# Weight sums a step earlier and on VectorE, a first operand in halves, and squares two steps later, in a decoder trunk on one core

## The chip, the cores and the metric

The kernel runs on one core of a Trainium2 chip. The metric is the device time of one execution in microseconds (us); three executions of the kernel before gave 2124.61, 2126.71 and 2128.39 us, so its median is 2126.71 us. The engines are named as the profile names them: PE (TensorE, PEld its weight loads), DVE (VectorE), ACT (ScalarE), POOL (GpSimd) and SP (SyncE, which issues most of the DMAs).

## The reference

Two layers on a stream `h` of 1024 tokens by 1024 features, all in float32: a gated short convolution with a feed-forward, then latent attention with a feed-forward, and a last norm.

```
def short_conv_mixer(h, w_in, conv_w, w_out):
    gate_b, gate_c, val = jnp.split(h @ w_in, 3, axis=-1)
    z = gate_c * val
    conv = sum(conv_w[k] * shifted(z, k) for k in range(3))
    return (gate_b * conv) @ w_out

def swiglu_ffn(h, w13, w2):
    g, u = jnp.split(h @ w13, 2, axis=-1)
    return (jax.nn.silu(g) * u) @ w2

h = h + short_conv_mixer(rms_norm(h), ...);  h = h + swiglu_ffn(rms_norm(h), ...)
h = h + latent attention(rms_norm(h), ...);  h = h + swiglu_ffn(rms_norm(h), ...)
return rms_norm(h, final_norm_g)
```

The attention turns queries and keys by tables `cos` and `sin` of the positions. `shifted` stands for the causal shift by k tokens.

## The kernel before

**Products.** Every matrix product in float32 is made of parts: an operand is split into a high part (a cast on ACT, L111) and a low part (operand less high part, a subtraction on DVE, L112), and three matmuls per tile (L153 to L155: high by high, low by high, high by low) give the product. Large products are further taken as 2 by 2 blocks by a scheme with seven block products in place of eight, whose operands are sums and differences of blocks. So between a loaded weight and the PE stand: a sum of blocks, a cast on ACT, a subtraction on DVE.

**Steps.** The order of all work is written by hand. `Steps` (L266) holds a list of PE steps; a step is one block product of 12 matmuls of 128x512. `before(n, ...)` puts other work ahead of step n and `after(n, ...)` behind it, and `run` emits all of it in that one order. Each engine takes its own instructions strictly in that order, and a wait for another engine holds up everything behind it on the same engine. SP's queue of DMAs is in order as well.

**Up products.** `up` (L487) plans the conv, and the two up projections of the feed-forwards, as `Quad`s of seven products. For a quad it loads two weight tiles `ra` and `rb`, splits one pair as it is (`pair_hi`, `pair_lo`), makes four sums in place (`sum3`, `sum1`, `sum2`, `sum4`, L386 to L396) and splits each by `half` (L398) two steps ahead of the product that reads it. Both `sum2` and `sum4` overwrite a buffer that an earlier half has read. The conv stage has 12 quads (three for each two of eight channel groups); seven of them (`head`) take their first two products ahead of the others, so that each has five steps in a row left. Its first product's operand comes from `block` and `first_block` (L918, L933): the PE transposes a normed tile into PSUM, DVE or ACT scales it (L927, L929), and the operand is split in pieces of 128x1024 (L316, L317). Results of a quad are folded from PSUM by DVE and ACT (`evict`, L445), multiplied and run through the three taps (L826 to L835) or gated (L843), on DVE.

**Down products.** `Down` (L656) makes the two down projections f1 and f2 as seven products of 11 k-tiles in groups of two; a group has its operands loaded (`load_m`, `load_w`) and split (`parts`, tiles mp and wp) two steps ahead of its first step. At the end of a product its four banks are added into the stream (L738), and where a piece of the stream is then complete, `complete` (L536) follows at once: in f1 it stores the piece and, for the second half of the later features, makes parts for the next stage; in f2 it makes the square for the last norm (L768), folds squares (L754) and applies the gain (L1598). In f2 the rows of the first half are normed and stored under the last products (`fnorm.flush`, `out_rows`, `out_turn`, `out_store`, L1657 to L1661).

**Tables.** Under f1's first products the rope tables are made, one small turn per step from step 6 of f1 on (L1153): for each half of the tokens a load of positions (L1093), a conversion (L1096), a reduction of the angle on DVE in some 16 turns, and last `sin` (L1106), which holds four DVE instructions, two sines on ACT (L1112, L1113), a negation on DVE (L1114) and two stores (L1115, L1116).

Of the kernel before, what the change touches and what calls it, by code (L numbers as in the profile page):

```python
# [10 lines left out]
F32R = mybir.dt.float32r  # L11
# [37 lines left out]
def trunk(ctx, tc, aps, out):  # L49
# [437 lines left out]
    def up(steps, quads, op, ahead=0):  # L487
# [20 lines left out]
        for x in quads:  # L508
# [16 lines left out]
            steps.before(n[x, 6] - 2, x.sum2, lambda x=x: x.half(6))  # L525
            steps.before(n[x, 7] - 2, lambda x=x: x.half(7))
            steps.before(n[x, 4] - 2, lambda x=x: x.half(4))
            steps.before(n[x, 3] - 2, x.sum4, lambda x=x: x.half(3))
# [127 lines left out]
    class Down:  # L656
# [12 lines left out]
        def product(self, steps, i):  # L669
# [66 lines left out]
            def evict(q, cb, t, sign):  # L736
                hv = st.h[cb * 4 + q][:, t * 512:(t + 1) * 512]
                nc.vector.tensor_tensor(hv, hv, banks[q], ALU.add if sign > 0 else ALU.subtract)  # L738
                if LAST[cb, t] == i:
                    complete(cb * 4 + q, t, self.final, self.keep)  # L740

            for j, o in enumerate(todo):
                steps.after(s - 3 + o[0] if tail else s + j // 2, lambda o=o: evict(*o))
# [78 lines left out]
    def conv_pair(j):  # L822
# [15 lines left out]
        return Quad(w_in, (KD + j) * P, (2 * KD + j) * P, AF.Copy, [product, first, tap(1), tap(2)], nc.gpsimd)  # L838

    def gate_pair(j):  # L840
        def done(i, c):
            y = kept[i]
            nc.vector.tensor_tensor(y, y, c, ALU.mult)  # L843
            if i < KD - 2:
                nc.sync.dma_start(md["conv"][i], y)
        return Quad(w_in, j * P, (j + 1) * P, AF.Copy, [lambda c1, c2: done(j, c1), lambda c1, c2: done(j + 1, c2)], nc.gpsimd)
# [89 lines left out]

    def first_x():
# [9 lines left out]
        first_block(0, 0)  # L947
# [14 lines left out]

    up(steps, conv_quads, xop)
    steps.before(1, lambda: first_block(1, 0), lambda: first_block(1, 1), xop.advance)
# [114 lines left out]
    def tables(hh):  # L1079
# [26 lines left out]
        def sin():  # L1106
# [4 lines left out]
            nc.vector.tensor_scalar(k, k, -1.0, float(np.pi / 2), ALU.mult, ALU.add)  # L1111
            nc.scalar.activation(x, a, AF.Sin)  # L1112
            nc.scalar.activation(a, k, AF.Sin)  # L1113
            nc.vector.tensor_scalar(x[64:128], x[64:128], -1.0, None, ALU.mult)  # L1114
# [7 lines left out]
        return out + [sin]  # L1122
# [30 lines left out]
    for j, fn in enumerate(tables(0) + tables(1)):  # L1153
        steps.before(dn.start + 6 + j, fn)
# [502 lines left out]
    steps.before(e[4] + 3, lambda: fnorm.flush(0))  # L1657
    steps.before(e[4] + 5, lambda: out_rows(0))
    for tb in range(4):
        for q in range(2):  # L1660
            steps.before(e[4] + 6 + (2 * tb + q + 1) // 2, lambda tb=tb, q=q: (out_turn(tb, q), out_store(tb, q)))  # L1661
# [43 lines left out]
```

## Time and profile before

| what | value |
| --- | --- |
| median of 3 runs (lowest, highest) | 2126.71 us (2124.61, 2128.39) |
| the profiled execution | 2122.53 us |
| its span | 2120.6 us |
| granted clock of PE, mean | 0.995 of full speed |
| PE, DVE, ACT, POOL busy | 97%, 69%, 40%, 15% of the span |
| chain of waits that ended last | PE 83%, DVE 7%, DMA 4%, ACT 3% |

The span is the profiled part of an execution; 1.9 us of its time lie around it. A share of busy time is a mean over stages: conv up from 0 to about 300 us, conv out to 380, f1's up to 787, f1's down to 997, attention to 1455, f2's up to 1880, f2's down to 2113. The bracket in a row of a timeline is the idle time of that engine ahead of the instruction and what ended it. A matmul of 128x512 lasts 0.39 us, and the next starts 0.23 us after it where nothing is late.

### The profile page before, as it was taken

How to read it: one execution, taken by the hardware profiler on the slowest of the kernel's cores; microseconds unless marked ns; L12 is line 12 of the kernel's file. 1: busy time of each engine (PE TensorE's matmuls, PEld its weight loads, DVE VectorE, ACT ScalarE, POOL GpSimd, SP SyncE). 2: the span in 40 equal slices, each digit the busy share in tenths (PEclk: the TensorE clock that was granted, in tenths of full speed). 3: DMA queues.
4: the chain of work that ended last, by engine and by line, in shares of the span. 5: the costliest groups of instructions: out<-in, count | busy, mean ns of one | idle time of the engine just before them, and what ended most of it. 6: DMA issues, size and time to landing. Idle time of an engine off the chain costs nothing.

```text
span 2120.6 us, 25572 instructions
## 1 busy us (share of the span) xinstructions
PE 2066.0 (97%) x9542; PEld 1706.4 (80%) x9542; DVE 1460.6 (69%) x2175; ACT 858.0 (40%) x1439; POOL 315.2 (15%) x412
## 2 busy tenths in 40 slices
PE   7999999999999999999999999989999999999998
PEld 6778888888888887787888888877888888888777
DVE  5787656887666668867577777437886666667555
ACT  7423434433333333354245555225433333333445
POOL 2233200122122210000023232101111111100000
PEclk9999999999999999999999999999999999999999
DMA  7255775586766586564232223325487475685543
GB/s 231 70 120 121 226 269 178 117 204 188 186 165 153 139 286 230 193 226 146 70 69 69 65 63 121 138 79 174 128 200 178 149 169 154 154 322 193 179 148 120
DMA packets 274315, 338.96 MB, mean 160 GB/s; under 512 B 18047, under 2 KB 177984, under 8 KB 273872
## 3 DMA queue, kind: packets, MB, share of 16 engines
q1 hardware_dynamic: 240144, 262.71, 38.1%
q0 software_dynamic: 33888, 74.56, 16.4%
q8 instruction: 74, 1.21, 0.2%
q14 instruction: 49, 0.40, 0.1%
q10 hardware_dynamic: 160, 0.07, 0.0%
HBM read 260.22 MB, written 126.35 MB: 182 GB/s over the span
## 4 chain that ended last, share of the span: by engine, by line
PE 83%; DVE 7%; DMA 4%; ACT 3%; issue 2%; SPq 0%; POOL 0%; DVEq 0%; ACTq 0%; POOLq 0%
PE q L154 16%; PE q L153 16%; PE q L155 16%; PE dn L155 4%; PE dn L154 4%; PE dn L153 4%; PE ps_s L1438 4%; PE pl L155 2%; PE pl L153 2%; PE pl L154 2%; DVE wp_lo L112 1%; PE ps_t L1460 1%; PE ps_l L155 1%; PE ps_l L153 1%; PE ps_l L154 1%
## 5 line engine op out<-in xcount | busy, mean ns | idle before, releaser
L153 PE MATMUL q<-xh,w_hi 128*128 128x512 f32 x1568 | 613.3, 391 | 6.3 <-ACT w_hi L111 2.6
L154 PE MATMUL q<-xl,w_hi 128*128 128x512 f32 x1568 | 611.5, 390 | 2.9 <-DVE xl L317 2.9
L155 PE MATMUL q<-xh,w_lo 128*128 128x512 f32 x1568 | 611.5, 390 | 0.9 <-DVE w_lo L112 0.9
L153 PEld LDWEIGHTS q<-xh,w_hi 128*128 128x128 f32 x1568 | 294.8, 188 | 70.6 <-ACT w_hi L111 3.8
L154 PEld LDWEIGHTS q<-xl,w_hi 128*128 128x128 f32 x1568 | 294.7, 188 | 65.9 <-DVE xl L317 4.8
L155 PEld LDWEIGHTS q<-xh,w_lo 128*128 128x128 f32 x1568 | 294.7, 188 | 63.2 <-DVE w_lo L112 2.4
L112 DVE TENSOR_TENSOR w_lo<-wr,w_hi 128x512 fp32r<-128x512 f32 (+1 forms) x272 | 196.6, 723 | 215.1 <-ACT w_hi L111 214.2
L111 ACT CAST w_hi<-wr 128x512 fp32r<-128x512 f32 (+1 forms) x272 | 170.1, 630 | 372.1 <-DVE wr L390 151.2
L155 PE MATMUL dn<-mp_hi,wp_lo 128*128 128x512 f32 (+1 forms) x628 | 245.3, 391 | 6.3 <-DVE wp_lo L112 4.5
L153 PE MATMUL dn<-mp_hi,wp_hi 128*128 128x512 f32 (+1 forms) x628 | 244.3, 389 | 1.0 <-ACT wp_hi L111 1.0
L154 PE MATMUL dn<-mp_lo,wp_hi 128*128 128x512 f32 (+1 forms) x628 | 243.3, 387 | 0.9 <-DVE mp_lo L112 0.9
L1050 POOL COPY paced<-pace 128x1 f32<-128x1 f32 x128 | 84.8, 663 | 923.0 <-ACT pace L1049 923.0
L112 DVE TENSOR_TENSOR mp_lo<-m,mp_hi 128x1024 fp32r<-128x1024 f32 x84 | 95.3, 1134 | 127.2 <-ACT mp_hi L111 125.6
L111 ACT CAST mp_hi<-m 128x1024 fp32r<-128x1024 f32 x84 | 82.2, 979 | 209.8 <-PE dn L154 204.0
L155 PEld LDWEIGHTS dn<-mp_hi,wp_lo 128*128 128x128 f32 x628 | 118.3, 188 | 38.8 <-DVE wp_lo L112 15.5
L153 PEld LDWEIGHTS dn<-mp_hi,wp_hi 128*128 128x128 f32 x628 | 118.3, 188 | 25.5 <-ACT wp_hi L111 2.8
L154 PEld LDWEIGHTS dn<-mp_lo,wp_hi 128*128 128x128 f32 x628 | 118.4, 188 | 25.5 <-DVE mp_lo L112 1.3
L112 DVE TENSOR_TENSOR wp_lo<-w,wp_hi 128x1024 fp32r<-128x1024 f32 x84 | 94.8, 1128 | 0.0
L111 ACT CAST wp_hi<-w 128x1024 fp32r<-128x1024 f32 x84 | 82.0, 976 | 0.0
L1445 ACT ACTIVATE p<-ps_s,mx,rq 128x128 f32<-128x128 f32 (+3 forms) x64 | 53.3, 834 | 56.6 <-DVE mx L1442 51.4
L382 DVE TENSOR_TENSOR w_lo<-wr,w_hi 128x1024 fp32r<-128x1024 f32 x56 | 68.7, 1226 | 7.6 <-ACT w_hi L378 7.6
L738 DVE TENSOR_TENSOR h<-h,dn 128x512 f32<-128x512 f32 x108 | 68.7, 679 | 0.0
(292 smaller groups left out, 3218.8 us busy)
## 6 DMA issues: line engine op xcount, KB each, us to landing
m<-md_f SPq DMA_DIRECT2D x70, 512.0 KB, 4.9
md_f<-c SPq DMA_DIRECT2D x110, 256.0 KB, 3.4
wr<-in_conv_ffn_w_dram SPq DMA_DIRECT2D x47, 512.0 KB, 5.7
wr<-in_mla_ffn_w_dram SPq DMA_DIRECT2D x47, 512.0 KB, 5.4
w<-mw_f SPq DMA_DIRECT2D x40, 512.0 KB, 3.9
h<-hd SPq DMA_DIRECT2D x32, 512.0 KB, 9.3
wr<-in_conv_w_in_dram SPq DMA_DIRECT2D x31, 512.0 KB, 5.2
mw_f<-in_conv_ffn_w_dram POOLq DMA_DIRECT2D x30, 512.0 KB, 7.2
```

What stands on the lines that cost most here:

```text
L111: nc.scalar.copy(out=hi, in_=src)
L112: (eng or nc.vector).tensor_tensor(lo, src, hi.bitcast(F32), ALU.subtract)
L153: nc.tensor.matmul(ps, lhsT=wh, rhs=xh, start=st, stop=False, **more)
L154: nc.tensor.matmul(ps, lhsT=wh, rhs=xl, start=False, stop=False, **more)
L155: nc.tensor.matmul(ps, lhsT=wl, rhs=xh, start=False, stop=en, **more)
L382: nc.vector.tensor_tensor(lo, self.ra, hi.bitcast(F32), ALU.subtract)
L738: nc.vector.tensor_tensor(hv, hv, banks[q], ALU.add if sign > 0 else ALU.subtract)
L1050: nc.gpsimd.tensor_copy(b, a)
L1438: nc.tensor.matmul(ps[:, a:b], lhsT=q[:, qs], rhs=k[:, a:b], start=i == 0, stop=i == 4)
L1445: nc.scalar.activation(p[:, :kw], ps[:, :kw], AF.Exp, bias=mx, scale=rq[:, qb:qb + 1], accum_out=rsum)
L1460: nc.tensor.transpose(t[:, j * P:(j + 1) * P], ps_[j][:, kb * P:(kb + 1) * P], ident)
```

## The change

It has five parts.

1. `up`: `sum2` and `sum4` stand a step earlier than the halves that they feed, in conv and in both feed-forwards (before: directly ahead of them). They run on DVE as before.
2. `conv_pair` and `gate_pair` (the same edit in both, the diff shows one): `sum3` and `sum1` of the conv stage run on DVE instead of POOL, and one step later (the step depends on the engine in `up`).
3. `first_halves` stands for the first `first_block`: the very first operand is scaled and split in two chunks of 128x512, one by one. The second pair of blocks, `first_block(1, 0)` and `(1, 1)`, is emitted ahead of the next quad's `pair_hi` in the same step.
4. `Down`: `complete` follows two steps behind the addition of a bank (not in the last product of f2), and the flush, rows, turns and stores of f2's first half move two steps later.
5. `tables`: the positions are loaded at steps 2 and 18 of f1 (before: in turn, at steps 6 and 24), and `sin` falls into three turns, a step each: the DVE instructions, the two sines on ACT, the negation with the stores.

```diff
-            steps.before(n[x, 6] - 2, x.sum2, lambda x=x: x.half(6))
+            steps.before(n[x, 6] - 3, x.sum2)
+            steps.before(n[x, 6] - 2, lambda x=x: x.half(6))
...
-            steps.before(n[x, 3] - 2, x.sum4, lambda x=x: x.half(3))
+            steps.before(n[x, 3] - 3, x.sum4)
+            steps.before(n[x, 3] - 2, lambda x=x: x.half(3))
...
-                if LAST[cb, t] == i:
+                if LAST[cb, t] == i and tail:
                     complete(cb * 4 + q, t, self.final, self.keep)
 
             for j, o in enumerate(todo):
-                steps.after(s - 3 + o[0] if tail else s + j // 2, lambda o=o: evict(*o))
+                n = s - 3 + o[0] if tail else s + j // 2
+                steps.after(n, lambda o=o: evict(*o))
+                if LAST[o[1], o[2]] == i and not tail:
+                    steps.after(n + 2, lambda o=o: complete(o[1] * 4 + o[0], o[2], self.final, self.keep))
...
-        return Quad(w_in, (KD + j) * P, (2 * KD + j) * P, AF.Copy, [product, first, tap(1), tap(2)], nc.gpsimd)
+        return Quad(w_in, (KD + j) * P, (2 * KD + j) * P, AF.Copy, [product, first, tap(1), tap(2)], nc.vector)
...
+    def first_halves():
+        b, hi, lo = slot("xraw"), slot("xh", F32R), slot("xl", F32R)
+        pts = [ps1("xps") for _ in range(2)]
+        for c, pt in enumerate(pts):
+            for tb in range(4):
+                nc.tensor.transpose(pt[:, tb * P:(tb + 1) * P], xt[tb][:, c * P:(c + 1) * P], ident)
+        for c, pt in enumerate(pts):
+            o = slice(c * 512, (c + 1) * 512)
+            if c == 0:
+                nc.vector.tensor_scalar(b[:, o], pt, gcol("conv_norm_g", c), None, ALU.mult)
+            else:
+                nc.scalar.activation(b[:, o], pt, AF.Copy, scale=gcol("conv_norm_g", c))
+            split(hi[:, o], lo[:, o], b[:, o])
+        xop.raw.setdefault((0, 0), {})[0] = b
+        xop.X.setdefault((0, 0), {})[0] = (hi, lo)
...
-        first_block(0, 0)
+        first_halves()
...
+    steps.before(1, lambda: first_block(1, 0), lambda: first_block(1, 1), xop.advance)
     up(steps, conv_quads, xop)
-    steps.before(1, lambda: first_block(1, 0), lambda: first_block(1, 1), xop.advance)
...
+        def store():
+            a, k, x = box["ang"], box["k1"], box["x"]
             nc.scalar.activation(x, a, AF.Sin)
             nc.scalar.activation(a, k, AF.Sin)
+
+        def negative():
+            a, x = box["ang"], box["x"]
             nc.vector.tensor_scalar(x[64:128], x[64:128], -1.0, None, ALU.mult)
...
-        return out + [sin]
+        return out + [sin, store, negative]
...
-    for j, fn in enumerate(tables(0) + tables(1)):
+    turns_ = [tables(hh) for hh in range(2)]
+    for hh in range(2):
+        steps.before(dn.start + 2 + 16 * hh, turns_[hh].pop(0))
+    for j, fn in enumerate(turns_[0] + turns_[1]):
         steps.before(dn.start + 6 + j, fn)
...
-    steps.before(e[4] + 3, lambda: fnorm.flush(0))
-    steps.before(e[4] + 5, lambda: out_rows(0))
+    steps.before(e[4] + 5, lambda: fnorm.flush(0))
+    steps.before(e[4] + 7, lambda: out_rows(0))
...
-            steps.before(e[4] + 6 + (2 * tb + q + 1) // 2, lambda tb=tb, q=q: (out_turn(tb, q), out_store(tb, q)))
+            steps.before(e[4] + 8 + (2 * tb + q + 1) // 2, lambda tb=tb, q=q: (out_turn(tb, q), out_store(tb, q)))
```

Lines behind 528 have other numbers in the changed kernel: L738 is L740 there, L768 is L773, L1093 is L1115, L1598 is L1629, and the two stores L1115 and L1116 are L1143 and L1144.

The first place is DVE in the conv stage, where the head quads begin to run one by one (about 86 us). In its rows `wr` is a weight tile, `w_lo` its low part, `c` a result tile, `xl` a low part of the stream's operand; L396 is `sum4`; L448, L467 and L469 fold PSUM banks into results. Before:

```order
L467 TENSOR_TENSOR c_682<-c_682 128x512
L396 TENSOR_TENSOR wr<-wr 128x512
L112 TENSOR_TENSOR w_lo<-wr,w_hi 128x512
L317 TENSOR_TENSOR xl<-xraw,xh 128x1024
L469 TENSOR_TENSOR c_634<-c_634,q 128x512
L396 TENSOR_TENSOR wr<-wr 128x512
L112 TENSOR_TENSOR w_lo<-wr,w_hi 128x512
L469 TENSOR_TENSOR c_682<-c_682,q 128x512
L112 TENSOR_TENSOR w_lo<-wr,w_hi 128x512
```

Now:

```order
L467 TENSOR_TENSOR c_684<-c_684 128x512
L112 TENSOR_TENSOR w_lo<-wr,w_hi 128x512
L396 TENSOR_TENSOR wr<-wr 128x512
L317 TENSOR_TENSOR xl<-xraw,xh 128x1024
L469 TENSOR_TENSOR c_637<-c_637,q 128x512
L112 TENSOR_TENSOR w_lo<-wr,w_hi 128x512
L387 TENSOR_TENSOR wr<-wr 128x512
L390 TENSOR_TENSOR wr<-wr 128x512
L469 TENSOR_TENSOR c_684<-c_684,q 128x512
L112 TENSOR_TENSOR w_lo<-wr,w_hi 128x512
L448 TENSOR_TENSOR c_279<-q,c_279 128x512
```

The second `sum4` (L396) stood directly ahead of the low part made from it; now another low part, the operand's part L317, L469 and a third low part stand between the sum and its own. The two sums L387 and L390 are new on DVE.

The second place is SP's queue under f1's third product (`m` and `w` are loads of a group, `rd` the table in memory, `rot` a table tile). Before:

```order
L678 DMA m<-md_f_92 128x2x512
L684 DMA w_6746<-mw_f_93 128x1024
L1115 DMA rd<-rot 128x512
L1116 DMA rd<-rot 128x512
L678 DMA m<-md_f_92 128x512
L1093 DMA rot<-in_positions_dram 128x512
L684 DMA w_6798<-mw_f_93 128x512
L678 DMA m<-md_f_92 128x2x512
```

Now:

```order
L680 DMA m<-md_f_92 128x2x512
L1115 DMA rot<-in_positions_dram 128x512
L686 DMA w_6668<-mw_f_93 128x1024
L680 DMA m<-md_f_92 128x2x512
L686 DMA w_6706<-mw_f_93 128x1024
L680 DMA m<-md_f_92 128x2x512
L686 DMA w_6755<-mw_f_93 128x1024
L680 DMA m<-md_f_92 128x512
L1143 DMA rd<-rot 128x512
L1144 DMA rd<-rot 128x512
L686 DMA w_6800<-mw_f_93 128x512
L680 DMA m<-md_f_92 128x2x512
```

The load of positions for the second half (L1093, now L1115) stood behind the two stores of the first half's table, and stands ahead of them now.

The third place is ACT at the end of f2's fourth product, where the first pieces of the stream are complete. Before:

```order
L111 CAST mp_hi<-m 128x1024
L111 CAST wp_hi<-w_16455 128x1024
L768 ACTIVATE nsq<-h 128x512
L1598 ACTIVATE h<-h,vec 128x512
L768 ACTIVATE nsq<-h 128x512
L1598 ACTIVATE h<-h,vec 128x512
L111 CAST mp_hi<-m 128x1024
L111 CAST wp_hi<-w_16491 128x1024
```

Now:

```order
L111 CAST mp_hi<-m 128x1024
L111 CAST wp_hi<-w_16457 128x1024
L111 CAST mp_hi<-m 128x1024
L111 CAST wp_hi<-w_16493 128x1024
L773 ACTIVATE nsq<-h 128x512
L1629 ACTIVATE h<-h,vec 128x512
L773 ACTIVATE nsq<-h 128x512
L1629 ACTIVATE h<-h,vec 128x512
L111 CAST mp_hi<-m 128x1024
L111 CAST wp_hi<-w_16529 128x1024
```

The squares (L768, now L773) and the gains (L1598, now L1629) stood ahead of the casts of the next group, and stand behind one more pair of casts now.

## Rows read from the trace of the kernel before

**Rows 1.** Section 1 of the page: busy us of each engine, share of the span, instructions.

```profile
PE 2066.0 (97%) x9542; PEld 1706.4 (80%) x9542; DVE 1460.6 (69%) x2175; ACT 858.0 (40%) x1439; POOL 315.2 (15%) x412
```

**Rows 2.** Windows view: us, busy us (x instructions) per engine, PEclk, DMA share, GB/s.

```profile
80.00:130.00 50.00, 44.73 (x182) 34.13 (x181) 43.01 (x52) 13.09 (x26) 17.33 (x16) 0.97 0.46 123
120.00:130.00 10.00, 8.21 (x29) 5.88 (x28) 8.26 (x12) 1.75 (x4) 1.89 (x2) 0.83 0.82 247
2040.00:2060.00 20.00, 17.42 (x78) 13.66 (x77) 11.60 (x19) 11.02 (x14) 0.00 (x0) 0.91 0.27 92
```

**Rows 3.** Timeline of PE, 86 to 130 us: start, us, instruction, [idle before <-releaser].

```profile
87.93 0.50 PE L153 MATMUL q<-xh,w_hi 128*128 128x512 f32 x1 [0.32 <-ACT w_hi L111]
...
93.28 0.50 PE L155 MATMUL q<-xh,w_lo 128*128 128x512 f32 x1 [0.85 <-DVE w_lo L112]
...
124.70 0.51 PE L153 MATMUL q<-xh,w_hi 128*128 128x512 f32 x1 [1.79 <-ACT w_hi L111]
```

**Rows 4.** Timeline of DVE, 86 to 93 us.

```profile
86.49 0.68 DVE L396 TENSOR_TENSOR wr<-wr 128x512 f32<-128x512 f32 x1
87.91 0.69 DVE L112 TENSOR_TENSOR w_lo<-wr,w_hi 128x512 fp32r<-128x512 f32 x1 [0.74 <-ACT w_hi L111]
88.52 1.22 DVE L317 TENSOR_TENSOR xl<-xraw,xh 128x1024 fp32r<-128x1024 f32 x1
89.66 0.68 DVE L469 TENSOR_TENSOR c<-c,q 128x512 f32<-128x512 f32 x1
...
91.67 1.55 DVE L112 TENSOR_TENSOR w_lo<-wr,w_hi 128x512 fp32r<-128x512 f32 x1 [0.74 <-ACT w_hi L111]
```

**Rows 5.** Timeline of POOL, 86 to 93 us.

```profile
91.41 1.27 POOL L387 TENSOR_TENSOR wr<-wr 128x512 f32<-128x512 f32 x1 [8.50 <-DMA wr<-in_conv_w_in_dram]
```

**Rows 6.** Lines view of POOL, 65 to 260 us: xcount | busy us, mean ns | idle before.

```profile
L390 POOL TENSOR_TENSOR wr<-wr 128x512 f32<-128x512 f32 x10 | 16.9, 1692 | 0.8
L387 POOL TENSOR_TENSOR wr<-wr 128x512 f32<-128x512 f32 x10 | 15.0, 1502 | 45.4 <-DVE w_lo L382 26.0 <-issue 10.5 <-DMA wr<-in_conv_w_in_dram 8.5
```

**Rows 7.** Timelines of PE (first two) and ACT (last), 14 to 38 us.

```profile
26.34 0.49 PE L153 MATMUL q<-xh,w_hi 128*128 128x512 f32 x1 [0.90 <-ACT xh L316]
27.61 0.50 PE L154 MATMUL q<-xl,w_hi 128*128 128x512 f32 x1 [0.77 <-DVE xl L317]
...
35.59 2.19 ACT L914 ACTIVATE xt<-xt,rs 128x1024 f32<-128x1024 f32 x2 [0.61 <-DVE rs L216]
```

**Rows 8.** Timelines of PE (three), ACT, SP queue and DVE, 836 to 863 us.

```profile
854.11 0.50 PE L153 MATMUL dn<-mp_hi,wp_hi 128*128 128x512 f32 x1 [0.47 <-ACT wp_hi L111]
...
855.56 0.50 PE L155 MATMUL dn<-mp_hi,wp_lo 128*128 128x512 f32 x1 [0.63 <-DVE wp_lo L112]
...
861.93 0.50 PE L154 MATMUL dn<-mp_lo,wp_hi 128*128 128x512 f32 x1 [0.86 <-DVE mp_lo L112]
...
849.82 0.64 ACT L1112 ACTIVATE rot<-rot 128x512 f32<-128x512 f32 x1 [5.69 <-DVE rot L1108]
...
853.57 0.40 SPq L1093 DMA_DIRECT2D rot<-in_positions_dram  x1
...
858.60 0.43 DVE L1096 CAST rot<-rot 128x512 f32<-128x512 int32 x1 [1.90 <-DMA rot<-in_positions_dram]
```

**Rows 9.** Timelines of ACT (two) and PE (four), 2000 to 2095 us.

```profile
2003.07 0.63 ACT L768 ACTIVATE nsq<-h 128x512 f32<-128x512 f32 x1 [2.07 <-DVE h L738]
...
2005.63 1.03 ACT L111 CAST mp_hi<-m 128x1024 fp32r<-128x1024 f32 x1
...
2009.12 0.50 PE L155 MATMUL dn<-mp_hi,wp_lo 128*128 128x512 f32 x1 [0.63 <-DVE wp_lo L112]
...
2049.13 1.05 PE L224 MATMUL sp<-ones,nsq 128*128 128x1 f32 x8 [1.95 <-DVE nsq L754]
...
2081.14 0.50 PE L155 MATMUL dn<-mp_hi,wp_lo 128*128 128x512 f32 x1 [0.21 <-DVE wp_lo L112]
...
2086.92 0.50 PE L153 MATMUL dn<-mp_hi,wp_hi 128*128 128x512 f32 x1 [0.49 <-ACT wp_hi L111]
```

More of the change, by code (lines that the diff above doesn't have):

```diff
@@ L845, in done @@
                 nc.sync.dma_start(md["conv"][i], y)
-        return Quad(w_in, j * P, (j + 1) * P, AF.Copy, [lambda c1, c2: done(j, c1), lambda c1, c2: done(j + 1, c2)], nc.gpsimd)
+        return Quad(w_in, j * P, (j + 1) * P, AF.Copy, [lambda c1, c2: done(j, c1), lambda c1, c2: done(j + 1, c2)], nc.vector)
     conv_quads = [f(*a) for j in range(0, KD, 2) for f, a in ((conv_pair, (j,)), (conv_pair, (j + 1,)), (gate_pair, (j,)))]
```

## The prediction

> **What bounds the kernel now.** I read the page's busy times first: PE works 2066.0 us, 97% of the span [rows 1]. So only time in which the PE stands, or runs at a lower clock, can be won, and the question is which of its waits this change touches. From the windows view and the bracketed rows of the PE's timeline I listed every wait of the PE by place. The stretch from 80 to 130 us has 44.73 busy in 50, so 5.27 idle, with the clock at 0.97; its last fifth has 0.83 [rows 2]. Six waits make up the 5.27: 0.32, 0.45, 0.85, 0.79, 1.07 and 1.79, of which three have their rows [rows 3]. Under f1 there are four, 0.47, 0.63, 0.86 and one more of 0.63, 2.59 in all [rows 8]. Under f2, from 2000 to 2095 us, there are eight: four of 0.63 or 0.64 (one has its row), 1.95, 0.49 and two of 0.21, 5.40 in all [rows 9], with the clock at 0.91 in the 20 us around the longest [rows 2].
>
> An idle time is not yet the loss. A matmul lasts 0.39 and the next starts 0.23 behind its start, so 0.16 of the matmul ahead goes with each wait, and the matmul behind it lasts 0.50; I add **0.2 a wait**, an estimate from these rows. The lower clock costs its share of the window: 0.17 of 10 us is 1.7, 0.09 of 20 us is 1.8 [rows 2]. Both falls of the clock, to the lower of its two levels (1.2 for 2.4 GHz), begin within 1 us of the end of the longest wait of their stretch, of 1.79 [rows 3] and of 1.95 [rows 9]; I take them to go with those waits.
>
> What stands to be won: conv 5.27 + 6 x 0.2 + 1.7 = **8.2**; f1 2.59 + 4 x 0.2 = **3.4**; f2 5.40 + 8 x 0.2 + 1.8 = **8.8**. The feed-forwards' up products have no such waits, so part 1 is worth nothing there: their DVE holds the sums either way, and its slack hides a step's move.
>
> **Part 1 and 2, conv.** The chain is in DVE's rows: sum4 starts at 86.49, the low part made from it at 87.91, after 0.74 of idle while ACT casts the sum [rows 4]. DVE is held by this each time, two times a quad. Now other DVE work stands in that place, so the 0.74 should go, and ACT gets its sum a step (2.7 us) earlier. One of the three named waits came otherwise: a low part took 1.55 instead of 0.69 [rows 4] while POOL's sum ran from 91.41 [rows 5]. POOL's sums last 1.27 to 1.7 [rows 5, 6]; the two on DVE stand for 0.61 each, since a 128x512 instruction's successor starts 0.61 behind it (87.91 to 88.52) and a 128x1024 one's 1.14 (88.52 to 89.66) [rows 4].
>
> Does DVE have the room? A head quad has five steps, 60 matmuls by 0.2275, 13.65 us of PE. DVE's share for it: five low parts, four sums and five folds of banks, 14 x 0.61 = 8.5; a product and two taps, 3 x 1.2 = 3.6; together 12.1. Before, without two sums but with two idle times of 0.74, it was 12.4, plus what POOL's sums lengthened. So DVE does a little better than before, although 24 sums, 14.6 us, come to it. Slack is 1.5 a quad, in places 0.4 by a walk through the new order with these durations, at the operand's last low parts and the low parts of two early quads. The sums read weights that land 5 us after issue and are now a step later, so nothing is late there; POOL's paced DMAs no longer stand behind sums. Bounds: 8.2 if all waits go, and a loss of up to 14.6 if DVE has no room (rivals). I take **7.2**, a wait of half a microsecond left in two places.
>
> The Trainium skill's page "Perfetto Trace Analysis", section "Optimizing Scalar/DVE Operations", speaks against this part: if DVE is saturated, it says, offloading some of its work, even to GpSimd, may make sense. It adds that the two share a read port, so that offloading between them might not help; the 1.55 row is of that second kind. By its first sentence the conv term would be the third rival's.
>
> **Part 3, start.** Step 2 waits 0.90 and 0.77 for parts that stood behind a weight cast which itself waited for a DMA [rows 7]; these go. But PE then comes earlier to the transposes of step 5, which need the second half's norms: ACT's scaling starts at 35.59 behind DVE's rs [rows 7], and that chain of four squares on ACT moves by 0.1 at most. And in product 0 the next block's scaling now stands on DVE behind two low parts that wait for casts, so it should end about 1.3 later than before, while its first matmul starts 0.7 sooner. Gated by the same chain, the sum is **0.1** won, between 0.7 won and 0.6 lost.
>
> **Part 5, f1.** ACT stood 5.69 for the first of DVE's four last instructions, and the casts behind the sines came late by it [rows 8]. Now DVE's four come one step earlier than the sines, ahead of a pair of evictions; the casts come about 1.9 sooner. The first two PE waits and their restarts (1.5) need that. The second pair comes from DVE waiting 1.90 for the positions, whose load was issued at 853.57 because SP's queue stood behind the table's stores [rows 8]; that load is now ahead of the stores, so this goes. The negation and stores are a step later, and SP's queue stands as long as before, with only loads behind it that were there before. I take **3.1** of 3.4, as the low part at 855.56 may still be 0.2 late; bounds 0 and 3.4.
>
> **Part 4, f2.** A square waits 2.07 for the eviction on DVE, and four instructions (0.65 apart) stand ahead of the cast at 2005.63 [rows 9]. Without them the cast starts when its data and buffer allow, some 3 us sooner, where PE lost 0.9. The squares run behind it, in ACT's slack. The 1.95 is the PE's wait for the last fold of squares [rows 9]; the rows' matmuls come two steps (5.4) later, the squares too, but the fold waits for one pair less. What is late next: the turns and stores of the first half now reach over the end of product 5, so that the banks of product 6 come free behind DVE's and ACT's stores; by the walk the fourth bank has 0.1 to 0.2 to spare. In f1 `complete` only stores, and nothing waits. I take **8.2** of 8.8; bounds 0 and 8.8.
>
> **Sum.** 7.2 + 0.1 + 3.1 + 8.2 = 18.6. The profiled execution took 2122.53 and would take 2103.9; the median of the runs stands 4.2 above it. The forecast is for a median: 2126.71 - 18.6 = **2108.1**.
>
> **Rivals.**
>
> *Conv stays bound by DVE.* The slack of 0.4 is used up where a DMA or a tap lengthens an instruction, a cast waits again, and the clock falls once more. For it: DVE was busy 43.01 of 50 in this stretch [rows 2]. Against: the idle times that go. Half of the conv term stays: +3.6, 2111.7.
>
> *f2's banks.* The stores under product 6 hold its banks, or the fold is still late by one wait and the clock falls again as before. For it: the 0.1 to 0.2 to spare. Against: the squares' 3 us. Half of 8.2 stays: +4.1, 2112.2. With the first rival, 2115.8.
>
> *DVE becomes the bound of the conv stage, and the kernel is slower.* If DVE needs more than 13.65 a head quad, each sum is paid in full: 24 x 0.61 = 14.6 more, and none of the 8.2 is won. It decides where the two cast waits (1.5) remain beside the 12.1: 13.6, at the edge, so any lengthening tips it. The other stages would win 11.4, so the kernel takes 2126.71 + 14.6 - 11.4 = 2129.9. Against: the sum stands a step ahead of its low part, with three to four DVE instructions between.
>
> *The start's halves do not do what they say.* Product 0 later by 1.3 and not hidden behind the norms' chain: 2109.5, inside the forecast's own spread.
>
> **How the numbers follow.** Forecast with its spread (2105 to 2110) 0.53, with the start's rival in it; conv half 0.18; f2 half 0.16; both 0.07; DVE as bound 0.03; the rest, a wait that I have not seen which eats nearly everything, 0.03. The runs before spread by 2 to either side. Low end: all terms in full, 20.4 and 0.7 at the start, is 2105.6, less 2: 2103.5. High end: both halves, 2115.8, and 2 more: 2118. A measurement can tell 0.2%, 4.25 us, from no change; faster means under 2122.5. Only the last two cases reach it: faster 0.94, same 0.03, slower 0.03.
>
> **What would show it.** In the stretch from 80 to 130 us PE busy over 49 of 50 with the clock at 1.00, DVE's idle for casts under 0.2 a time, POOL without sums, no low part of 1.55. Under f1 no PE wait over 0.3 from 850 to 865, and positions issued long before their conversion. At f2's fourth and fifth products casts ahead of squares, the rows' matmuls without a wait. Wrong would be: PE waits for w_lo in the conv stage with DVE busy without a gap, or a new PE wait at product 6's first matmuls for a store.

## The result

The changed kernel took 2098.46 us (median of four runs, 2095.37 to 2103.7) against 2125.66 for the kernel before (2122.12 to 2128.39): a ratio of 0.9876, with an interval of 0.9847 to 0.9904. It is **faster by 27 us**, the forecast was 18.6 faster, and 2098.46 lies below the stated range. A second measurement of the same two kernels, with the experiments below, gave 2100.97 against 2123.74, a ratio of 0.9902 (0.9886 to 0.9918), 22.8 us. That time lies below the range as well; the kernel before took 3.0 us less there than the 2126.71 from which the forecast was counted. Both count in what follows: the gain is about 22.5 us in the stages that the change touches, and in the profiles of the first measurement 4.5 more in the attention stage, whose instructions it leaves alone.

The page of the changed kernel (span 2093.7, profiled execution 2095.82), busy times, against [rows 1]:

```profile
PE 2053.9 (98%) x9542; PEld 1704.7 (81%) x9542; DVE 1463.5 (70%) x2200; ACT 855.7 (41%) x1440; POOL 269.4 (13%) x388
```

PE's busy time fell by 12.1 although its matmuls are the same: a matmul beside a wait or under the lower clock lasts longer, and there are fewer of these. The stages in us, each from its first matmul to that of the next (the start goes to the last transpose of the first operand, f1's and f2's down products to the end of their last matmul):

| stage | before | changed | forecast of the difference | difference |
| --- | --- | --- | --- | --- |
| start | 57.4 | 57.4 | -0.1 | 0.0 |
| conv's up products behind it | 211.6 | 202.4 | -7.2 | -9.2 |
| conv out and f1's up products | 512.0 | 512.1 | 0 | +0.1 |
| f1's down products | 217.2 | 214.5 | -3.1 | -2.7 |
| attention, with its in and out products | 460.1 | 455.6 | 0 | -4.5 |
| f2's up products | 422.4 | 422.4 | 0 | 0.0 |
| f2's down products | 230.5 | 219.9 | -8.2 | -10.6 |

The windows view of the changed kernel in conv and around the sums for the rows of f2's first half (the stretch begins 159.3 us behind f2's first down product, as before), against the first and third of [rows 2]:

```profile
80.00:130.00 50.00, 50.00 (x222) 41.43 (x221) 48.67 (x67) 17.17 (x33) 8.98 (x14) 1.00 0.64 147
2023.80:2043.80 20.00, 20.00 (x103) 16.78 (x102) 11.43 (x19) 9.66 (x13) 0.00 (x0) 1.00 0.36 119
```

PE is busy 50.00 of 50 at full clock, where it was 44.73 at 0.97, and 20.00 of 20, where it was 17.42 at 0.91. In conv DVE went from 43.01 to 48.67. Its timeline shows the chain taken apart, against [rows 4]:

```profile
86.50 0.68 DVE L396 TENSOR_TENSOR wr<-wr 128x512 f32<-128x512 f32 x1
87.10 1.22 DVE L317 TENSOR_TENSOR xl<-xraw,xh 128x1024 fp32r<-128x1024 f32 x1
88.24 0.68 DVE L469 TENSOR_TENSOR c<-c,q 128x512 f32<-128x512 f32 x1
88.84 0.68 DVE L112 TENSOR_TENSOR w_lo<-wr,w_hi 128x512 fp32r<-128x512 f32 x1
89.44 0.68 DVE L387 TENSOR_TENSOR wr<-wr 128x512 f32<-128x512 f32 x1
90.16 0.69 DVE L390 TENSOR_TENSOR wr<-wr 128x512 f32<-128x512 f32 x1
```

Between the sum L396 at 86.50 and its own low part at 88.84 stand the operand's part and a fold. (The buffers of the rows show it so; the section on the change named one low part too many there, and the third rival "three to four" instructions: it is two here, and one to three at the next sums.) Two are enough for ACT's cast: DVE does not stand still, and each instruction lasts what it lasts alone. Where only one stands between, at 98.15, DVE waits 0.15; its longest wait for a cast from 80 to 130 us is 0.22, where it was 0.69 to 1.24 seven times. The two sums of part 2 (L387, L390) are the last two rows.

Under f1 the sines (now L1137, L1138) stand on ACT as before, but 1.85 earlier, counted from f1's first matmul (66.95 behind it, before 68.80); these are ACT's and then PE's bracketed rows, against [rows 8]:

```profile
838.93 0.63 ACT L1137 ACTIVATE rot<-rot 128x512 f32<-128x512 f32 x1 [3.89 <-DVE rot L1130]
840.64 0.63 ACT L1138 ACTIVATE rot<-rot 128x512 f32<-128x512 f32 x1 [1.08 <-DVE rot L1133]
```

```profile
845.26 0.50 PE L155 MATMUL dn<-mp_hi,wp_lo 128*128 128x512 f32 x1 [0.25 <-DVE wp_lo L112]
...
851.36 0.50 PE L155 MATMUL dn<-mp_hi,wp_lo 128*128 128x512 f32 x1 [0.35 <-DVE wp_lo L112]
```

ACT waits 3.89 for DVE instead of 5.69, and of the four PE waits of 0.47 to 0.86 two are left, of 0.25 and 0.35; the prediction's sign for this part was none over 0.3. Which of the part's halves, the earlier load or the sines in turns, gives how much was not tried. DVE's conversion of the second positions waits for nothing now. At f2's fourth product ACT's order is the one that the change wrote, against [rows 9]:

```profile
1985.41 1.05 ACT L111 CAST mp_hi<-m 128x1024 fp32r<-128x1024 f32 x1 [0.71 <-PE dn L154]
1986.36 1.05 ACT L111 CAST wp_hi<-w 128x1024 fp32r<-128x1024 f32 x1
1987.31 0.63 ACT L773 ACTIVATE nsq<-h 128x512 f32<-128x512 f32 x1
1987.97 0.72 ACT L1629 ACTIVATE h<-h,vec 128x512 f32<-128x512 f32 x1
```

The casts at 1985.41 and 1986.36 are through before the first square; no PE wait above 0.14 is left there.

### The profile page after: what moved, and what is told of

It reads as the page before. It is cut to its first block, busy times and chain, and to the rows that moved or that the text cites. A ratio compares the mean times of both kernels' runs of the same rounds, so it can differ in the third digit from the quotient of the medians.

```text
span 2093.7 us, 25560 instructions
## 1 busy us (share of the span) xinstructions
PE 2053.9 (98%) x9542; PEld 1704.7 (81%) x9542; DVE 1463.5 (70%) x2200; ACT 855.7 (41%) x1440; POOL 269.4 (13%) x388
## 4 chain that ended last, share of the span: by engine, by line
PE 88%; DVE 6%; ACT 2%; issue 2%; DMA 1%; DVEq 0%; SPq 0%; ACTq 0%
PE q L154 17%; PE q L155 17%; PE q L153 17%; PE dn L155 5%; PE dn L153 5%; PE dn L154 5%; PE ps_s L1469 4%; PE pl L153 2%; PE pl L155 2%; PE pl L154 2%; DVE wp_lo L112 1%; PE ps_t L1491 1%; PE ps_l L155 1%; PE ps_l L153 1%; PE ps_l L154 1%
## 5 line engine op out<-in xcount | busy, mean ns | idle before, releaser
L112 DVE TENSOR_TENSOR w_lo<-wr,w_hi 128x512 fp32r<-128x512 f32 (+1 forms) x272 | 191.9, 705 | 199.3 <-ACT w_hi L111 197.5
L153 PE MATMUL dn<-mp_hi,wp_hi 128*128 128x512 f32 (+1 forms) x628 | 242.9, 387 | 0.0
L1072 POOL COPY paced<-pace 128x1 f32<-128x1 f32 x128 | 75.1, 587 | 1020.4 <-ACT pace L1071 1020.4
L473 ACT ACTIVATE c<-c 128x512 f32<-128x512 f32 x44 | 27.8, 632 | 131.7 <-DVE c L448 131.7
## 6 DMA issues: line engine op xcount, KB each, us to landing
m<-md_f SPq DMA_DIRECT2D x70, 512.0 KB, 4.9
wr<-in_conv_ffn_w_dram SPq DMA_DIRECT2D x47, 512.0 KB, 6.3
wr<-in_mla_ffn_w_dram SPq DMA_DIRECT2D x47, 512.0 KB, 5.4
w<-mw_f SPq DMA_DIRECT2D x40, 512.0 KB, 3.9
h<-hd SPq DMA_DIRECT2D x32, 512.0 KB, 9.6
wr<-in_conv_w_in_dram SPq DMA_DIRECT2D x31, 512.0 KB, 5.7
mw_f<-in_conv_ffn_w_dram POOLq DMA_DIRECT2D x30, 512.0 KB, 7.7
```

What stands on the lines that cost most here:

```text
L112: (eng or nc.vector).tensor_tensor(lo, src, hi.bitcast(F32), ALU.subtract)
L153: nc.tensor.matmul(ps, lhsT=wh, rhs=xh, start=st, stop=False, **more)
L473: nc.scalar.activation(self.C1[:, 512:], self.C1[:, 512:], self.first)
L1072: nc.gpsimd.tensor_copy(b, a)
```

## The experiments

All but the last four take the changed kernel and undo one piece of it. Medians are of four runs each; the runs of one group share the runs of the kernel before, whose medians lay between 2123.66 and 2127.36. The lengths of stages come from the profiles and are much finer than the medians: conv's, f1's and f2's stages repeat to 0.1 us where their code is the same. So the sizes below go by the stages; a median stands against the first measurement of the changed kernel, 2098.46, which is 2.5 below the second. (The expectations give conv's stage from 62 us on, 197.8, or from the first product, 242.9; the last transpose, on which 202.4 rests, proved the steadier mark.)

**Part 4 undone.**

```diff
-                if LAST[cb, t] == i and tail:
+                if LAST[cb, t] == i:
...
-    steps.before(e[4] + 7, lambda: out_rows(0))
+    steps.before(e[4] + 5, lambda: out_rows(0))
```

> The changed kernel with part 4 undone: squares, gains and folds directly behind the additions again, f2's first rows, turns and stores two steps earlier again. Theory (each stage stands by itself): f2's stage, 229.3 us from its first matmul to the end in the changed kernel and 239.9 before, goes back to about 239, with waits of 0.63 at the fourth and fifth product, one of 1.95 for the last fold and a fall of the clock behind it; the whole time is 9 to 11 us above the changed kernel's. Rival (the gain of f2 hangs on earlier stages, or half of it is the luck of one run's clock): 5 us or less.

It took 2109.22, 10.8 above the changed kernel (8.3 above its second measurement). f2's stage is 230.5 again, as before to 0.1; the other touched stages are unchanged (conv 202.4, f1 214.5), so in f1 the part gives nothing.

**Parts 1 and 2 undone.**

```diff
-            steps.before(n[x, 6] - 3, x.sum2)
+            steps.before(n[x, 6] - 2, x.sum2)
...
-        return Quad(w_in, ..., [product, first, tap(1), tap(2)], nc.vector)
+        return Quad(w_in, ..., [product, first, tap(1), tap(2)], nc.gpsimd)
```

> The changed kernel with parts 1 and 2 undone: two sums on POOL again, the other two directly ahead of their low parts again. Theory: the stage from the first product to the end of conv's up products, 242.9 us in the changed kernel and 252.2 before, goes back to about 252; the six waits between 85 and 125 us are there again; 8 to 10 us above the changed kernel. Rival (the start's new order carried part of it): under 6.

2107.66, 9.2 above (6.7 above the second measurement). conv's stage is 211.6 again, with six waits, and the windows view has the old row:

```profile
80.00:130.00 50.00, 44.91 (x182) 34.27 (x181) 42.84 (x53) 13.27 (x26) 17.35 (x16) 0.97 0.46 124
```

**Part 5 undone** (`sin` in one turn, loads of positions at steps 6 and 24).

> The changed kernel with part 5 undone: positions loaded at steps 6 and 24 of f1, the sines in one turn with the rest. Theory: f1's stage, 214.8 us in the changed kernel and 217.6 before, goes back by 2.5 to 3.5 us, with the four waits of 0.47 to 0.86 there again, and the attention stage (from f1's last matmul to the first of f2's up products, 455.9 in the changed kernel, 460.3 before) does not follow: it varies from run to run with the clock's falls alone. Rival: the attention's 4.4 us come from the tables standing earlier; then the whole time rises by about 7.

2099.52. f1's stage went from 214.5 to 217.2, the value before. PE's waits are there again:

```profile
844.72 0.50 PE L153 MATMUL dn<-mp_hi,wp_hi 128*128 128x512 f32 x1 [0.46 <-ACT wp_hi L111]
...
846.17 0.50 PE L155 MATMUL dn<-mp_hi,wp_lo 128*128 128x512 f32 x1 [0.64 <-DVE wp_lo L112]
...
852.60 0.50 PE L154 MATMUL dn<-mp_lo,wp_hi 128*128 128x512 f32 x1 [0.88 <-DVE mp_lo L112]
853.74 0.50 PE L155 MATMUL dn<-mp_hi,wp_lo 128*128 128x512 f32 x1 [0.63 <-DVE wp_lo L112]
```

The attention stage was 455.8, as short as in the changed kernel, so it does not hang on the tables; with the median only 1.1 above the first measurement and 1.5 below the second, a part of 2.7 us is at the edge of what four runs can tell.

**Part 3 undone** (`first_block(0, 0)` again, the second blocks behind the next quad's cast).

> The changed kernel with part 3 undone: first operand in one piece, second blocks behind the next quad's cast. Theory: the transposes of the second half wait for the norms' chain in either order, so the time changes by less than 1 us either way; step 2 waits 0.90 and 0.77 again, and the wait near 35 us is shorter by as much. Rival: the first products end later by 1 to 2 us and the whole with them.

2099.83; the start took 57.6, against 57.4 and 57.6 in the two profiles of the changed kernel. Of the two waits of step 2 that were expected back only the one of 0.76 came. The changed kernel waits at other places, and longest for the transposes of the second half; first its PE rows, then those of the undone one:

```profile
19.85 0.50 PE L153 MATMUL q<-xh,w_hi 128*128 128x512 f32 x1 [1.06 <-ACT xh L316]
21.11 0.50 PE L154 MATMUL q<-xl,w_hi 128*128 128x512 f32 x1 [0.76 <-DVE xl L317]
...
36.45 0.90 PE L929 MATMUL xps<-ident,xt 128*128 128x128 f32 x3 [1.08 <-DVE xt L921]
```

```profile
27.86 0.50 PE L154 MATMUL q<-xl,w_hi 128*128 128x512 f32 x1 [0.76 <-DVE xl L317]
...
36.67 0.90 PE L929 MATMUL xps<-ident,xt 128*128 128x128 f32 x3 [0.24 <-DVE xt L921]
```

The wait for the norms' scaling is 1.08 in the one and 0.24 in the other: what is won ahead of it is waited there. (In four profiles with part 3, the changed kernel's second one among them, it is 0.28 to 0.58; in these the clock fell between 21 and 23 us, in the first products.) The first matmul did not start sooner in the changed kernel's first profile (16.64, before 16.50), where the clock had fallen ahead of it; in five later profiles in which that came later or not at all it started at 15.3 to 15.8, the 0.7 of the prediction or more. The start took 57.1 in the two of them without a fall, as the profile of before had none, and 57.4 to 57.9 in the other three. So the part is worth 0.3 at most, and with one profile of each kernel that is not shown either.

**One half of conv at a time.** Part 2 alone undone (two sums on POOL):

> The changed kernel with part 2 alone undone: the first two sums of a conv quad on POOL, a step earlier; the other two still a step ahead of their low parts. conv's stage (first product to last) is 242.9 us in the changed kernel, 252.0 with both parts undone. Theory (contention and the wait for the cast both hold DVE; each part alone gives a share): the waits of 0.32, 0.45 and 0.79 go, but a low part beside a POOL sum still takes 1.5 and one or two waits of 0.5 to 1.0 stay; 2 to 5 us above the changed kernel. Rival (the step ahead does it all, POOL's sums are harmless): within 1 us of the changed kernel.

2102.80; conv's stage is 204.9, 2.5 longer. Two PE waits remain, 0.71 and 1.20, and the first shows what POOL does: its two sums, and then DVE's instructions of the same time.

```profile
94.57 1.30 POOL L387 TENSOR_TENSOR wr<-wr 128x512 f32<-128x512 f32 x1
95.94 1.64 POOL L390 TENSOR_TENSOR wr<-wr 128x512 f32<-128x512 f32 x1
```

```profile
94.35 2.08 DVE L393 TENSOR_TENSOR wr<-wr 128x512 f32<-128x512 f32 x1
96.35 1.78 DVE L112 TENSOR_TENSOR w_lo<-wr,w_hi 128x512 fp32r<-128x512 f32 x1
```

A sum of 0.68 took 2.08 and a low part of 0.69 took 1.78. In the whole of conv's stage no sum or low part of 128x512 on DVE lasted over 0.69 unless a POOL sum ran beside it, and with one beside it up to 2.08. No POOL sum ran beside the second wait, at 121.44 for a low part, but two ran from 108.26 to 111.79, and beside them DVE lost 2.1 us:

```profile
108.86 1.79 DVE L112 TENSOR_TENSOR w_lo<-wr,w_hi 128x512 fp32r<-128x512 f32 x1
110.57 2.31 DVE L840 SCALAR_TENSOR_TENSOR conv<-c,vec,conv 128x1023 f32<-128x1023 f32 x1
```

From there to the low part at 120.70 DVE worked without a gap, so the loss came through to the PE. Part 1 alone undone (sum2 and sum4 directly ahead of their low parts):

> The changed kernel with part 1 alone undone: sum2 and sum4 directly ahead of their low parts; all four sums of conv on DVE. Theory: DVE stands 0.7 twice a quad for the cast and has 24 sums more than before, 12.1 + 1.5 = 13.6 of 13.65 us a quad, so the waits of 85 to 125 us are there and more of them; 8 to 15 us above the changed kernel. Rival (POOL's contention was the cause, the step does little): under 3 us above.

2105.64, conv's stage 207.2, 4.8 longer. The theory's size was too large: three waits, not more than six, with DVE busy 44.18 of 50.

```profile
88.43 0.50 PE L153 MATMUL q<-xh,w_hi 128*128 128x512 f32 x1 [0.33 <-ACT w_hi L111]
...
92.20 0.50 PE L153 MATMUL q<-xh,w_hi 128*128 128x512 f32 x1 [0.45 <-ACT w_hi L111]
...
122.13 0.50 PE L153 MATMUL q<-xh,w_hi 128*128 128x512 f32 x1 [1.81 <-ACT w_hi L111]
```

So contention and order each held the stage: 2.5 us for the one and 4.8 for the other, 7.3 together; both undone cost 9.2, which is 7.5 and 1.7 for the clock's fall (half of the 3.4 us at the lower level). The windows row of this run has the clock at 1.00 in spite of the wait of 1.81:

```profile
80.00:130.00 50.00, 47.41 (x201) 36.65 (x200) 44.18 (x62) 15.08 (x30) 7.78 (x11) 1.00 0.52 131
```

**One half of f2 at a time.** Only rows, turns and stores two steps earlier:

> The changed kernel with only f2's flush, rows, turns and stores two steps earlier again, squares still two steps behind their additions. Theory: the fold then waits for squares that have just been issued, so the PE's wait for the rows (1.95 before) is there again and longer, 2 to 5 us, and the clock may fall behind it (1.7); the waits of 0.63 stay away; 4 to 7 us above the changed kernel. Rival: the squares' move is all that counts, within 1 us.

2100.89, f2's stage 221.2, 1.3 longer; the theory fell. No wait for the fold came back. The cost is that the rows' sums then read two tiles of squares, with 16 matmuls in place of 8, and a wait of 0.14 stands 25 us behind them; the row of this run, then that of the changed kernel:

```profile
2031.79 1.84 PE L224 MATMUL sp<-ones,nsq 128*128 128x1 f32 x16
```

```profile
2032.55 0.95 PE L224 MATMUL sp<-ones,nsq 128*128 128x1 f32 x8
```

Only the squares, gains and folds directly behind their additions:

> The changed kernel with only the squares, gains and folds directly behind their additions again; rows, turns and stores of f2's first half stay two steps later. Theory: the waits of 0.63 at the fourth, fifth and sixth product are there again, six of them or so at about 1.1 each with the slower matmuls around them, and the wait of 1.95 is gone; f2's stage is 5 to 7 us above the changed kernel's 219.9. Rival (ACT's squares cost little by themselves, the rows' wait and the clock's fall are the gain): 3 us or less.

2108.27, f2's stage 227.9, 8.0 longer, a little above the theory. The waits of 0.63 came back, six of 0.60 to 0.64 in all; the first two:

```profile
1997.29 0.50 PE L155 MATMUL dn<-mp_hi,wp_lo 128*128 128x512 f32 x1 [0.63 <-DVE wp_lo L112]
...
2003.92 0.50 PE L155 MATMUL dn<-mp_hi,wp_lo 128*128 128x512 f32 x1 [0.64 <-DVE wp_lo L112]
```

So the squares' move is worth 8.0 of f2's 10.6; the rows' move is worth 2.6 while the squares stand early, 1.7 of it the clock.

**The changed kernel again.**

> The changed kernel once more, unaltered. Theory: conv's, f1's and f2's stages repeat to 0.5 us (197.8 behind the first 62 us, 214.5, 219.9), and only the start and the attention stage differ (452 to 455 plus 1.7 for every fall of the clock), so its median lies between 2096 and 2102; what stood above the three stages' 22.5 us in the first comparison is the clock in stages that the change does not touch. Rival (the change also lowers the attention's falls): the attention stage is 456 us or less again, as in the first profile, where the kernels with a part undone had 456 to 460.

2100.97. Conv 202.4, f1 214.5, f2 219.9: they repeat. The attention stage was 461.5, longer than in any other profile and 5.9 longer than in the first profile of the same kernel; the third column from the right of these windows rows is the clock. First the changed kernel's first profile, then this one, then the kernel before:

```profile
987.00:1442.00 455.00, 436.45 (x2306) 370.19 (x2307) 294.42 (x617) 193.96 (x376) 85.56 (x115) 1.00 0.30 88
```

```profile
994.00:1455.00 461.00, 441.97 (x2304) 374.13 (x2303) 296.10 (x618) 194.48 (x377) 85.59 (x115) 0.98 0.30 90
```

```profile
998.00:1458.00 460.00, 440.01 (x2307) 372.54 (x2306) 294.50 (x616) 194.42 (x377) 85.63 (x115) 0.99 0.30 87
```

The granted clock is 1.00, 0.98 and 0.99 there. In the first profile of the changed kernel 3.4 us of the stage ran at the lower level, in the second 20.5, before 10.2. The 17.1 us more made the stage 5.9 longer, so here they cost a third of their time, and not the half that the prediction took for conv and f2. The rival (the change lowers the falls in attention) is out. But the kernel before also has a wait there, at its first scores, that none of the thirteen later profiles has:

```profile
1096.68 0.33 PE L1438 MATMUL ps_s<-kh,qnh 128*128 128x128 f32 x1 [1.41 <-DVE vl L112]
```

From it on PE is 1.4 to 1.6 behind the others. So about 1.5 of the 4.5 is this wait and most of the rest goes with the clock; whether the change takes the wait away, or one execution had it, a single profile of the kernel before can't tell.

**How much room DVE has in conv.** The low part of each conv quad's first sum, then three of its low parts (`(5, 6, 7)` in place of `(5,)`), made twice:

```diff
             split(hi[:, o:o + 512], lo[:, o:o + 512], src)
+            if self.first == AF.Copy and i in (5,):
+                nc.vector.tensor_tensor(lo[:, o:o + 512], src, hi[:, o:o + 512].bitcast(F32), ALU.subtract)
```

> The changed kernel, and in each of conv's 12 quads the low part of its first sum is made twice (one DVE instruction of 128x512 more, the result is the same). It asks how much room DVE has in conv. Theory by the count of the prediction: 12.1 + 0.6 = 12.7 of 13.65 us a quad, so DVE has room, and no wait over 0.7 comes: conv's stage behind 62 us stays within 1.5 us of 197.9. Rival by the busy share (DVE 48.67 of 50 us busy from 80 to 130 us in the changed kernel): DVE is full there, four quads pay 0.6 each and more for the waits, 3 to 6 us longer.

2101.88; conv's stage 203.5, 1.1 longer, with one wait of 0.43.

> As the run with one low part twice, with three low parts of each quad made twice (1.8 us of DVE a quad more). By the count: 12.1 + 1.8 = 13.9 of 13.65, so DVE is the bound wherever a quad has five steps in a row; conv's stage is 2 to 8 us longer with many waits for low parts. By the busy share: 1.8 for each of some seven quads, 10 to 16 us longer.

2105.63; conv's stage 211.1, 8.7 longer: a little more than the count said, less than the busy share said. Two windows rows, with one low part twice and with three:

```profile
80.00:130.00 50.00, 49.57 (x218) 40.36 (x217) 48.77 (x69) 15.59 (x30) 8.76 (x12) 1.00 0.59 137
```

```profile
80.00:130.00 50.00, 46.07 (x192) 34.93 (x192) 48.78 (x68) 15.75 (x28) 7.52 (x10) 1.00 0.54 131
```

DVE is busy 48.77 and 48.78 of 50, as in the changed kernel (48.67), while PE goes from 50.00 by 49.57 to 46.07. The busy share does not tell the three apart; the count per quad does: 12.7 of 13.65 fits but for that one wait, 13.9 does not.

**A version beyond the change.** At the start of each down product after the first, the changed kernel's PE comes late by 0.30: 0.53 from one start to the next where 0.23 is usual, and 0.34 to the one behind.

```profile
802.12 0.39 PE L154 MATMUL dn<-mp_lo,wp_hi 128*128 128x512 f32 x1
802.65 0.50 PE L155 MATMUL dn<-mp_hi,wp_lo 128*128 128x512 f32 x1
802.99 0.40 PE L153 MATMUL dn<-mp_hi,wp_hi 128*128 128x512 f32 x1
```

The group ahead has a single k-tile, so that PE needs 2.7 us for it, and the parts of the next group take longer from the release of their buffers. With those parts made k-tile by k-tile:

```diff
-                    for key in ("m", "w"):
-                        hi, lo = hi_tile(key + "p_hi")[:, :n], lo_tile(key + "p_lo")[:, :n]
-                        split(hi, lo, box[key])
-                        box[key + "p"] = (hi, lo)
+                    for key in ("m", "w"):
+                        box[key + "p"] = hi_tile(key + "p_hi")[:, :n], lo_tile(key + "p_lo")[:, :n]
+                    width = 512 if g == 0 and i > 0 else n
+                    for c in range(0, n, width):
+                        for key in ("m", "w"):
+                            hi, lo = box[key + "p"]
+                            split(hi[:, c:c + width], lo[:, c:c + width], box[key][:, c:c + width])
```

> The changed kernel, and in the down products the parts of the first group of products 2 to 7 made k-tile by k-tile (each pair of casts and low parts as two of 128x512 in place of one of 128x1024), so that the low part of the weight's first tile is there earlier. Theory: the wait of 0.14 at the start of each such product, 0.41 with the slower matmuls around it, goes: 5 in f1 and 5 in f2, about 4 us off the time. Rival: eight small instructions instead of four cost ACT and DVE 0.15 each more and only move the wait to the group's second tile; no change within 1 us.

2096.50 against 2100.97 for the changed kernel on the same chip; its ratio to the kernel before is 0.9873 (0.9852 to 0.9894), the changed kernel's 0.9902 (0.9886 to 0.9918). These intervals overlap, but the stages tell it: f1 went from 214.5 to 212.2 and f2 from 219.9 to 217.7, 4.5 us together, where about 4 was expected: there were eleven such starts, six in f1 and five in f2, not ten. It is the fastest version measured here.

## Why the prediction was wrong in size

**The mechanisms held, part by part.** Each stage stands by itself: undoing part 4 gave 10.6 back in f2, parts 1 and 2 gave 9.2 in conv, part 5 gave 2.7 in f1, part 3 nothing. Most of what was forecast as the sign of each was there: no PE wait in conv, casts ahead of squares, rows without a wait, POOL without sums. Two signs were missed by little: an idle time of DVE for a cast of 0.22 (under 0.2 was forecast) and a PE wait of 0.35 under f1 (none over 0.3). None of the rivals came. The run with part 1 alone undone stands at the edge that the third rival names, 13.6 of 13.65, and cost 4.8 us, where the rival had 14.6 beside the 8.2 not won.

**The step that failed is the price of a wait, "I add 0.2 a wait".** Measured, six waits with 5.27 of idle in conv cost 7.46 of PE time (clock apart): 0.37 a wait on top of its idle time. In f2 nine waits with 5.5 of idle cost 8.9, again 0.37. Both gains, 9.2 and 10.6, lie above what the prediction gave as bounds, 8.2 and 8.8. Where it goes is in the starts: around a wait of 0.63 the starts are 0.34 instead of 0.23 apart one matmul ahead of it and again one behind it, besides the 0.16 that I counted. Rows of the kernel before, first in f2 and then in conv:

```profile
2007.67 0.50 PE L153 MATMUL dn<-mp_hi,wp_hi 128*128 128x512 f32 x1
2008.01 0.47 PE L154 MATMUL dn<-mp_lo,wp_hi 128*128 128x512 f32 x1
2009.12 0.50 PE L155 MATMUL dn<-mp_hi,wp_lo 128*128 128x512 f32 x1 [0.63 <-DVE wp_lo L112]
2009.45 0.40 PE L153 MATMUL dn<-mp_hi,wp_hi 128*128 128x512 f32 x1
```

```profile
100.92 0.39 PE L155 MATMUL q<-xh,w_lo 128*128 128x512 f32 x1
102.09 0.50 PE L153 MATMUL q<-xh,w_hi 128*128 128x512 f32 x1 [0.79 <-ACT c L460]
102.42 0.39 PE L154 MATMUL q<-xl,w_hi 128*128 128x512 f32 x1
```

The starts give 1.16 for the wait of 0.63 and 1.05 for that of 0.79. So 0.37 is a mean of two kinds: 0.27 on top where only the matmul behind is late, 0.53 where its neighbours are late too. The three waits of the run with part 1 undone are of the second kind, and by the starts 2.59 of idle cost 4.2 there. Even the wait of 0.14 at a product's start, which I took as nothing, costs 0.41. With 0.37 the ceilings would have been 9.2 for conv, 10.2 for f2 and 4.1 for f1 from the same rows (conv and f2 gave the figure, f1 is a check of it); f1's two waits that stayed, 0.25 and 0.35, keep 1.3 of the last, which leaves 2.8 for the 2.7 measured.

**The second is the discount.** I took 1.0 off conv and 0.6 off f2 for waits that might remain. None remained in conv: DVE's count of 12.1 a quad was right and the 0.4 in the narrow places was enough. In f2 the same: the stores under product 6 held no bank up, and the small waits after it went too. The two errors make conv 2.0 and f2 2.4 too small, f1 0.4 too large: 22.5 instead of 18.6. (Some 0.4 of f2's is a ninth wait, of 0.14, that the prediction did not list.) From the median of that time this is 2104.2, inside the range.

**The third put it outside the range.** I let all other stages stand as they were, a term put at nothing with no row behind it, and gave the runs 2 us to either side. The attention stage, with the same instructions in the same order, lay between 455.5 and 461.5 in the fourteen profiles, mostly by how much of it ran at the lower clock: 3.4 us in the shortest, 20.5 in the longest. In the first comparison the stage fell by 4.5 in the changed kernel's favour in the profile (about 1.5 of it by the wait of 1.41), and the four runs of that kernel spread by 8.3, 2095.37 to 2103.7. The fall of the clock was also tied too firmly to its wait. In f2 it came behind the wait of 1.95 in both profiles that had that wait. In conv it came behind the wait of 1.79 in two profiles, and not behind one of 1.81 in a third; nor did it come with eleven waits of 5.1 in all, the longest of 1.24 (three low parts made twice). So of the 22.5 us the 3.4 for the two falls are what these profiles show, not a constant.

**On the rival that speaks for POOL.** The Trainium skill's page "Perfetto Trace Analysis", section "Optimizing Scalar/DVE Operations", says that offloading, even to GpSimd, may make sense where DVE is saturated, and adds that the two share a read port, so that it might not help. Here the second sentence decides: with its sums on POOL DVE was busy 47.69 of 50 in conv with 57 instructions, nearly as much as with the sums and 67 instructions (48.67), since POOL's sums lengthened DVE's own instructions to 2.08 and 1.78, and the stage was 2.5 us longer. That the slowing goes through the port no run here shows; that it goes with POOL's sums they do. What the first sentence would have given, conv bound by DVE, came only with 1.8 us more a quad.

## What to carry to other kernels

Where PE is the bound, price each of its short waits at its idle time and 0.3 to 0.5 us more, read from the distances of the starts around it and not from the brackets; small waits that look like nothing (0.14) then add up to a version of its own. Whether an engine has room for more work is told by a count of its instructions per unit of the pipeline against PE's time for the same unit, by the distances of starts; its busy share was the same with room and without. And before a difference of some microseconds is explained, look at a stage that the change does not touch: here it moved by up to 6 from one profile to the next.

## What the runs showed that was not expected

A wait of the PE slows its neighbours: the matmul one ahead of it and the one behind start 0.34 after their predecessors instead of 0.23. DVE at 97% of its time did not hold PE up at all. And the up products of f1, with no wait in the profile of before, had one of 1.2 to 1.7 us in three of the fourteen profiles, the changed kernel's second one among them; in all three ACT's copy of a bank (L460) waited 3.1 to 3.3 us for a store that still read its tile. In the run with parts 1 and 2 undone:

```profile
447.66 0.60 ACT L460 ACTIVATE c<-q 128x512 f32<-128x512 f32 x1 [3.27 <-DMA md_f<-c]
```

What makes the clock fall in attention little in one execution and much in the next was not tried and stays open.
